# Half-head scores between projections, a later fill, routing copies on VectorE, and index digits in PSUM

## The chip, the core and the metric

The program runs on one core of a Trainium2 chip. TensorE (PE in the profile) multiplies matrices, its weight loads have a row of their own (PEld); VectorE (DVE) and ScalarE (ACT) work element by element and can read and write PSUM, where TensorE leaves its sums; GpSimd (POOL) works on SBUF, and it also issues the gathers by index; SyncE (SP) issues most of the plain loads. Each engine takes its instructions in the order of its own queue and waits on semaphores for the others. The metric is the time of one execution on the device, in microseconds (us).

## The reference

One layer of an encoder block over 512 tokens of width 1024, in float32. A mixing part (a spatial gating group beside a banded attention group) is added to the input. Then comes PEER, a product-key mixture of 16384 one-row experts. It is the second part that the change touches:

```python
q = (xb @ w_query).reshape(PEER_TOKEN_BLOCK, PEER_HEADS, 2, PEER_HALF)
sc = jnp.einsum('thpd,hpkd->thpk', q, sub_keys).astype(jnp.float32)
s_top, i_top = lax.top_k(sc, PEER_TOPK)
cand = s_top[:, :, 0, :, None] + s_top[:, :, 1, None, :]
cand_idx = i_top[:, :, 0, :, None] * PEER_NKEYS + i_top[:, :, 1, None, :]
best, pos = lax.top_k(cand.reshape(...), PEER_TOPK)
eidx = jnp.take_along_axis(cand_idx.reshape(...), pos, axis=-1)
g = jax.nn.softmax(best, axis=-1)
h = jax.nn.gelu(jnp.einsum('thkd,td->thk', expert_u[eidx], xb))
return jnp.einsum('thk,thkd->td', g * h, expert_v[eidx])
```

For each token and each of 8 heads a query of two halves is scored against two sets of 128 keys. The 16 best keys of each half give candidate pairs, and the 16 best pairs name 16 experts of that head, with a softmax gate for each.

## The kernel before

The tokens are four tiles of 128. One tile is handled by gathering the rows of its experts. The other three are handled densely: every expert's product with every token is made on TensorE in 128 blocks of 128 experts, and multiplied by a gate matrix that is zero where an expert was not chosen. Float32 operands are split into a high part `hi` (a rounded copy, by ScalarE) and a rest `lo` (a subtraction, by VectorE or GpSimd), and a product is three matmuls (`mm3`). For 64 of the dense tokens the first products are not made densely either; their expert rows are gathered early (`gather_early`, tile `rowe`) and reduced by VectorE (`dots_early`, called dots below).

The program has four stages after one another: the mixing part, the routing, the gate steps, and the second products with the gathered tile beside them. The change touches the routing and the gate steps.

**Routing** (the loop over `h` after `candidates`). For head `h` the weights of the query are loaded and split (two `lo` on GpSimd), and TensorE makes the projection of both halves (48 matmuls of 512 columns). Then come `FILL[h]` blocks of first products (24 matmuls of 320 columns each, one `lo` on GpSimd each), the first of them ahead of the scores. Then come the scores of both halves in one go, and ScalarE copies them out (`scr`, `s0`). VectorE finds the 16 best of each half for three token tiles (`top16` in `best_keys`). One round later `pairs` forms the candidates, with three small copies on ScalarE for heads 0 to 5 and on VectorE for heads 6 and 7, and `choose` takes the 16 best pairs and looks their indices up through six bit masks in PSUM and a tree of predicated copies, which ends in `eidx`. Two rounds after a head's scores GpSimd casts its indices and issues six gathers. After head 7 come eight more blocks of first products (`BRIDGE`), the softmax of all gates, and `indices_of`, which takes the index digits of one tile apart in integer arithmetic in SBUF (`ii`) and writes them back as floats. A scheduler that works by priority and readiness sets the order on each engine here; `issue_after` only adds edges.

**Gate steps** (the loop `for n in range(steps + LEAD)`, an order written out by hand). Each of 48 steps handles 8 tokens: `second_one_hot` on GpSimd makes `bm`, `first_one_hot` on VectorE makes `am`, and two steps later TensorE multiplies them (`products`). ScalarE copies the product to `gst`, and every second step a 1 MB store to DRAM follows. Between them stand a quarter of a block of first products per step, dots, gathers, splits (`split_next`, two of three on VectorE and the third on GpSimd), and twice `indices_of` for the next token tile. `gates_of` transposes the digits and gates on TensorE into a PSUM bank that VectorE reads for 16 steps.

PSUM tiles `pa` share four banks in both stages, and `pu`, for the first products, has two.

Of the kernel before, what the change touches and what calls it, by code (L numbers as in the profile page):

```python
# [8 lines left out]
F32 = mybir.dt.float32  # L9
# [62 lines left out]
FILL = (2, 2, 2, 2, 3, 3, 3, 3)  # L72
# [20 lines left out]
def hybrid_block(tc, x, ln1, w_in, gng, wsT, bsb, qkg, bias, w_out, ln2, wq, skT, uT, ud, vd, out):  # L93
    nc = tc.nc
    ctx = ExitStack()
    with ctx:
# [18 lines left out]
        iota_k = const.tile([P, P], F32, name="iota_k")  # L115
        nc.gpsimd.iota(iota_k, pattern=[[1, P]], base=0, channel_multiplier=0,
# [610 lines left out]
        def top16(val, pos, src, scratch):  # L727

            nc.vector.max(val[:, 0:8], src)
            nc.vector.max_index(pos[:, 0:8], val[:, 0:8], src)  # L730
            nc.vector.match_replace(scratch, val[:, 0:8], src, LOW)
            nc.vector.max(val[:, 8:16], scratch)
            nc.vector.max_index(pos[:, 8:16], val[:, 8:16], scratch)
# [6 lines left out]
        def best_keys(pool, top, pos, u, p2, src):  # L740
            rep = pool.tile([P, NK], F32, name="rep", tag="rep", bufs=2)
            top16(top[:, 0, u, p2, :], pos[:, u, p2, :], src, rep)
# [26 lines left out]
        def choose(pool, cand, n, best, to, mask, tree, spread=nc.gpsimd.tensor_copy):  # L769
# [7 lines left out]
            for i in range(6):  # L777
                nc.vector.tensor_scalar(mask[:, i * n * TOPK:(i + 1) * n * TOPK], bpos.rearrange("p t k -> p (t k)"),
                                        1 << i, None, op0=ALU.bitwise_and)
            mask = mask.rearrange("p (l t k) -> p l t k", t=n, k=TOPK)  # L780
            for i in reversed(range(6)):
# [20 lines left out]

        def candidates(h):

            if h:
                w = chunk_of(wq, h, eng=nc.gpsimd)
            else:
                with queued_behind(behind_norm):
                    w = chunk_of(wq, h)
            skt = rq.tile([P, 2, NK], F32, name="skt", tag="skt", bufs=2)  # L810
            nc.sync.dma_start(skt, skT[:, 2 * h:2 * h + 2, :])
            top, pos = keys(rq, ND)
            qts = []
            for p2 in range(2):
                ps = pa()
                for k in range(KT):
                    mm3(ps, w(k, slice(p2 * P, (p2 + 1) * P)), (xbh[:, k, :], xbl[:, k, :]),
                        k == 0, k == KT - 1)
                qt = rq.tile([P, S], F32, name="qt", tag="qt", bufs=2)
                nc.scalar.copy(qt, ps)  # L820
                qts.append(qt)
            fill = first_products(sum(FILL[:h]) + BC, FILL[h], nc.gpsimd, True)
            next(fill, None)
            s0 = rq.tile([P, 2, NK], F32, name="s0", tag="s0", bufs=2)
            for p2 in range(2):
                sp = pa()
                for t in range(TT):
                    nc.tensor.matmul(sp[:, t * P:(t + 1) * P], qts[p2][:, t * P:(t + 1) * P],
                                     skt[:, p2, :], start=True, stop=True)
                sc = rq.tile([P, ND, NK], F32, name="scr", tag="scr", bufs=2)  # L830
                nc.scalar.copy(sc, sp.rearrange("p (t n) -> p t n", n=NK)[:, GT:, :])
                nc.scalar.copy(s0[:, p2, :], sp[:, 0:NK])
                for t in range(ND):
                    best_keys(rq, top, pos, t, p2, sc[:, t, :])
            nc.scalar.dma_start(s0d[h], s0.rearrange("p a n -> p (a n)"))
            for _ in fill:
                pass
            return top, pos


        def indices_of(t):

            ii = gat.tile([P, 3, NH * TOPK], I32, name="ii", tag="ii", bufs=1)
            ff = ii.bitcast(F32)
# [4 lines left out]
            nc.vector.tensor_scalar(ei, ei, BL - 1, None, op0=ALU.bitwise_and)  # L849
            nc.vector.tensor_copy(ff, ii)  # L850
# [10 lines left out]
        cands = []  # L861
        for h in range(NH + 1):
            dots_early(0)
            if h < NH:
                cands.append(candidates(h))
            else:
# [358 lines left out]
```

## Time and profile before

| | |
|---|---|
| median of 3 runs | 1438.37 us (1434.36 to 1438.52) |
| profiled execution, own time | 1439.93 us |
| its span, first to last instruction | 1438.1 us |
| granted TensorE clock, mean | 0.990 |
| PE, DVE, POOL, ACT busy in the span | 1395.6, 1160.8, 703.3, 612.3 us |
| routing, 224 to 454 us: PE, DVE, POOL busy | 217.17, 185.59, 167.89 of 230 us |
| gate steps, 454 to 610 us: PE, DVE, POOL busy | 135.20, 131.93, 122.07 of 156 us |
| second products, from 610 us: PE busy | 822.84 of 828.1 us |

Rows of a timeline read: start, duration, engine, line, operation, output and inputs, shapes, count, and in brackets the idle time of the engine just before with what ended it. Rows of a table of groups give the count after an x, then the busy time and the mean of one in ns, then the idle time before. Rows of a table of waits give the time in total, how often, and the longest. Records of neighbouring instructions overlap a little, since an engine starts one while the last drains; so what an instruction costs in a row of its kind is the distance from start to start.

### The profile page before, as it was taken

How to read it: one execution, taken by the hardware profiler on the slowest of the kernel's cores; microseconds unless marked ns; L12 is line 12 of the kernel's file. 1: busy time of each engine (PE TensorE's matmuls, PEld its weight loads, DVE VectorE, ACT ScalarE, POOL GpSimd, SP SyncE). 2: the span in 40 equal slices, each digit the busy share in tenths (PEclk: the TensorE clock that was granted, in tenths of full speed). 3: DMA queues.
4: the chain of work that ended last, by engine and by line, in shares of the span. 5: the costliest groups of instructions: out<-in, count | busy, mean ns of one | idle time of the engine just before them, and what ended most of it. 6: DMA issues, size and time to landing. Idle time of an engine off the chain costs nothing.

```text
span 1438.1 us, 21787 instructions
## 1 busy us (share of the span) xinstructions
PE 1395.6 (97%) x7838; PEld 1233.5 (86%) x7838; DVE 1160.8 (81%) x2558; ACT 612.3 (43%) x975; POOL 703.3 (49%) x479
## 2 busy tenths in 40 slices
PE   9999999999988897899999999999999999999998
PEld 7887788998988887899898899898998998888887
DVE  5537753688999989689999999899879888688883
ACT  5447635443433444554434444343433333333331
POOL 0002104588778897514454556556545455254520
PEclk9999999999999999999999999999999999999999
DMA  4452226478667997879799999999989989789981
GB/s 164 129 191 74 89 103 206 137 263 280 230 212 233 300 326 231 272 264 351 285 354 360 335 351 367 346 399 363 388 328 360 358 328 366 260 328 352 350 325 62
DMA packets 164331, 396.25 MB, mean 276 GB/s; under 512 B 12880, under 2 KB 75232, under 8 KB 162176
## 3 DMA queue, kind: packets, MB, share of 16 engines
q1 hardware_dynamic: 64640, 194.14, 37.6%
q0 software_dynamic: 48176, 173.46, 32.9%
q10 hardware_dynamic: 51408, 27.27, 6.5%
q8 instruction: 61, 1.00, 0.3%
q14 instruction: 46, 0.38, 0.1%
HBM read 363.34 MB, written 31.46 MB: 275 GB/s over the span
## 4 chain that ended last, share of the span: by engine, by line
PE 74%; DVE 13%; DMA 6%; ACT 3%; POOL 2%; issue 2%; POOLq 0%; ACTq 0%; DVEq 0%; SPq 0%
PE pa L1145 21%; PE px L1145 11%; PE pu L189 9%; PE pu L190 9%; PE pu L191 9%; PE pa L189 4%; PE pa L190 3%; PE pa L191 3%; DMA gd<-gst 3%; DVE lo L152 2%; PE pa L956 2%; DVE row L1086 1%; DVE am L948 1%; DMA gc<-gd 1%; DVE acc L1097 1%
## 5 line engine op out<-in xcount | busy, mean ns | idle before, releaser
L151 ACT ACTIVATE hi<-raw 128x1024 fp32r<-128x1024 f32 x296 | 312.5, 1058 | 443.7 <-DMA raw<-in_vd 116.0
L152 DVE TENSOR_TENSOR lo<-raw,hi 128x1024 fp32r<-128x1024 f32 x243 | 302.7, 1247 | 79.8 <-ACT hi L151 79.2
L1084 POOL DMA_INDIRECT row<-in_ud,eint x128 | 199.5, 1559 | 172.7 <-DVE acc L1097 107.4
L1095 POOL DMA_INDIRECT row<-in_vd,eint x128 | 185.6, 1450 | 172.3 <-DVE row L1086 120.7
L189 PE MATMUL pu<-xch,hi 128*128 128x320 f32 x784 | 247.5, 316 | 1.2 <-ACT act L713 1.2
L190 PE MATMUL pu<-xcl,hi 128*128 128x320 f32 x784 | 242.5, 309 | 0.0
L191 PE MATMUL pu<-xch,lo 128*128 128x320 f32 x784 | 242.1, 309 | 0.0
L1145 PE MATMUL pa<-hi,wh 128*128 128x512 f32 x512 | 199.8, 390 | 0.0
L1145 PE MATMUL pa<-lo,wh 128*128 128x512 f32 x512 | 199.3, 389 | 0.0
L152 POOL TENSOR_TENSOR lo<-raw,hi 128x1024 fp32r<-128x1024 f32 x53 | 126.5, 2405 | 92.9 <-ACT hi L151 92.1
L1097 DVE SCALAR_TENSOR_TENSOR acc<-row,hw,acc 128x1024 f32<-128x1024 f32 x128 | 164.9, 1288 | 1.4 <-DMA row<-in_vd,eint 1.2
L1086 DVE SCALAR_TENSOR_TENSOR row<-row,xb 128x1024 f32<-128x1024 f32 x128 | 157.5, 1233 | 2.3 <-DMA row<-in_ud,eint 2.3
L1145 PE MATMUL pa<-hi,wl 128*128 128x512 f32 x512 | 158.2, 389 | 0.0
L189 PEld LDWEIGHTS pu<-xch,hi 128*128 128x128 f32 x784 | 148.3, 189 | 4.3 <-ACT act L713 2.9
L190 PEld LDWEIGHTS pu<-xcl,hi 128*128 128x128 f32 x784 | 148.3, 189 | 1.5
L191 PEld LDWEIGHTS pu<-xch,lo 128*128 128x128 f32 x784 | 148.1, 189 | 0.0
L956 PE MATMUL pa<-bm,am 128*128 128x128 f32 x768 | 99.0, 282 | 16.4 <-DVE am L948 8.7
L1145 PEld LDWEIGHTS pa<-hi,wl 128*128 128x128 f32 x512 | 96.1, 188 | 20.4
L1145 PEld LDWEIGHTS pa<-hi,wh 128*128 128x128 f32 x512 | 96.1, 188 | 20.3
L1145 PEld LDWEIGHTS pa<-lo,wh 128*128 128x128 f32 x512 | 96.1, 188 | 20.1
L956 PEld LDWEIGHTS pa<-bm,am 128*128 128x128 f32 x768 | 94.1, 197 | 20.6 <-issue 9.1
L1145 PE MATMUL px<-hi,wh 128*128 128x512 f32 x256 | 100.7, 393 | 4.2 <-ACT hi L151 4.2
(236 smaller groups left out, 2661.1 us busy)
## 6 DMA issues: line engine op xcount, KB each, us to landing
raw<-in_uT SPq DMA_DIRECT2D x128, 512.0 KB, 5.6
raw<-in_vd SPq DMA_DIRECT2D x128, 512.0 KB, 6.1
gd<-gst ACTq DMA_DIRECT2D x24, 1024.0 KB, 7.5
gc<-gd SPq DMA_DIRECT2D x15, 1280.0 KB, 8.5
raw<-in_w_in SPq DMA_DIRECT2D x19, 512.0 KB, 4.4
raw<-in_wq SPq DMA_DIRECT2D x16, 512.0 KB, 3.6
raw<-in_w_out SPq DMA_DIRECT2D x8, 512.0 KB, 3.6
gc<-gd SPq DMA_DIRECT2D x15, 256.0 KB, 10.3
```

The source lines that it names most:

```text
L151: nc.scalar.activation(hi, raw, AF.Copy)
L152: ins = eng.tensor_tensor(lo, raw, hi.bitcast(F32), op=ALU.subtract)
L189: nc.tensor.matmul(ps, lh[0], rh[0], start=first, stop=False)
L190: nc.tensor.matmul(ps, lh[0], rh[1], start=False, stop=False)
L191: nc.tensor.matmul(ps, lh[1], rh[0], start=False, stop=last)
L948: nc.vector.tensor_tensor(am, iota_k[:, None, :].to_broadcast(full), g[:, 0, c * TC:(c + 1) * TC, None].to_broadcast(full), op=ALU.is_equal)
L956: nc.tensor.matmul(ps[:, i * P:(i + 1) * P], am[:, 4 * q + i, :], bm[:, 4 * q + i, :], start=True, stop=True)
L1084: nc.gpsimd.indirect_dma_start(out=row, out_offset=None, in_=ud, in_offset=bass.IndirectOffsetOnAxis(ap=eint[:, j:j + 1], axis=0))
L1086: nc.vector.scalar_tensor_tensor(row, row, 1.0, xb0, op0=ALU.mult, op1=ALU.mult, accum_out=hw[:, j:j + 1])
L1095: nc.gpsimd.indirect_dma_start(out=row, out_offset=None, in_=vd, in_offset=bass.IndirectOffsetOnAxis(ap=eint[:, j:j + 1], axis=0))
L1097: nc.vector.scalar_tensor_tensor(acc0, row, hw[:, j:j + 1], acc0, op0=ALU.mult, op1=ALU.add)
L1145: nc.tensor.matmul(accs[t][half], (wh, wh, wl)[k][:, b, tok], w[b][k % 2][:, ds_], start=first and k == 0, stop=last and k == 2)
```

## The change

The code of routing is cut into two generators: `projected_keys(h, p2)` makes the projection of half a head and pauses in its middle, and `best_of(h, p2)` makes that half's scores and its 16 best keys. `candidates(h)` puts the scores of the half before into that pause: those of head `h-1`, half 1, amid the projection of head `h`, half 0, and those of half 0 amid the projection of half 1. Only the last head's second half has a block of first products in between. `scr` gets four buffers instead of two. The fill goes from two blocks per head, then three, to 0, 1, 2, 3, 4, 4, 3, 3, the sum being 20 as before. The dots of a round are queued behind that round's last `top16`. The copies of `pairs` are on VectorE for all heads. The six bit masks, one `tensor_scalar` each, become one `tensor_tensor` of `bpos` with a constant tile `bits`; this holds for the gathered tile too, where `choose` runs once per head. `indices_of` works in a PSUM bank and writes floats to a tile of its own. In the gate steps nothing is split in steps 0 and 1, and in steps 2 to 5 GpSimd makes all splits.

```diff
-FILL = (2, 2, 2, 2, 3, 3, 3, 3)
+FILL = (0, 1, 2, 3, 4, 4, 3, 3)
...
-            for i in range(6):
-                nc.vector.tensor_scalar(mask[:, i * n * TOPK:(i + 1) * n * TOPK], bpos.rearrange("p t k -> p (t k)"),
-                                        1 << i, None, op0=ALU.bitwise_and)
             mask = mask.rearrange("p (l t k) -> p l t k", t=n, k=TOPK)
+            nc.vector.tensor_tensor(mask, bpos[:, None, :, :].to_broadcast([P, 6, n, TOPK]),
+                                    bits[:, :, None, None].to_broadcast([P, 6, n, TOPK]), op=ALU.bitwise_and)
...
+            ps = pa()
+            for k in range(KT):
+                if k == KT // 2:
+                    yield
+                mm3(ps, weights_q[h](k, slice(p2 * P, (p2 + 1) * P)), (xbh[:, k, :], xbl[:, k, :]),
+                    k == 0, k == KT - 1)
...
+            sc = rq.tile([P, ND, NK], F32, name="scr", tag="scr", bufs=4)
+            nc.scalar.copy(sc, sp.rearrange("p (t n) -> p t n", n=NK)[:, GT:, :])
...
             for p2 in range(2):
+                for _ in projected_keys(h, p2):
+                    if p2:
+                        best_of(h, 0)
+                    elif h:
+                        best_of(h - 1, 1)
             fill = first_products(sum(FILL[:h]) + BC, FILL[h], nc.gpsimd, True)
+            if h == NH - 1:
+                next(fill, None)
+                best_of(h, 1)
...
-            ii = gat.tile([P, 3, NH * TOPK], I32, name="ii", tag="ii", bufs=1)
-            ff = ii.bitcast(F32)
+            ii = pa()[:, 0:3 * NH * TOPK].bitcast(I32).rearrange("p (i k) -> p i k", i=3)
...
+            ff = gat.tile([P, 3, NH * TOPK], F32, name="ff", tag="ff", bufs=1)
...
-            dots_early(0)
             if h < NH:
-                cands.append(candidates(h))
+                candidates(h)
+            with queued_behind(found):
+                dots_early(0)
...
-                    cand = pairs(rq, *cands.pop(0), ND, ps[:, 6 * ND * TOPK:8 * ND * TOPK], h >= NH - 1)
+                    cand = pairs(rq, *top_pos.pop(h - 1)[:2], ND, ps[:, 6 * ND * TOPK:8 * ND * TOPK], True)
...
-                while split < (AHEAD - LAST) * BC + HELD and len(ready) < HELD:
-                    split_next(nc.vector if split % 3 else nc.gpsimd)
+                if n > 1 and split < (AHEAD - LAST) * BC + HELD and len(ready) < HELD:
+                    split_next(nc.vector if split % 3 and n > 5 else nc.gpsimd)
```

Three places show how the order moves. The first is VectorE at the end of the choice of a middle head, where the masks are made (`bpos` holds the positions of the best pairs, `tree` the indices being looked up, the rows at L659 are dots). Before:

```order
L778 TENSOR_SCALAR pa<-bpos 128x48 x5
L659 SCALAR_TENSOR_TENSOR rowe,du<-rowe,px 128x1024
L778 TENSOR_SCALAR pa<-bpos 128x48
L788 COPY_PREDICATED tree<-pa,cand 128x48x18
L659 SCALAR_TENSOR_TENSOR rowe,du<-rowe,px 128x1024
L788 COPY_PREDICATED tree<-pa,tree 128x48x16
L659 SCALAR_TENSOR_TENSOR rowe,du<-rowe,px 128x1024
L788 COPY_PREDICATED tree<-pa,tree 128x48x8
```

And now, lines being three further down:

```order
L736 MAX_INDEX bpos<-gate,rep_2421 128x8
L781 TENSOR_TENSOR pa<-bpos,bits 128x288
L790 COPY_PREDICATED tree<-pa,cand 128x48x18
L790 COPY_PREDICATED tree<-pa,tree 128x48x16
L790 COPY_PREDICATED tree<-pa,tree 128x48x8
L790 COPY_PREDICATED tree<-pa,tree 128x48x4
L790 COPY_PREDICATED tree<-pa,tree 128x48x2
L790 COPY_PREDICATED tree<-pa,tree 128x48
L792 COPY eidx<-tree 128x3x16
```

Six masks became one instruction, and for heads 0 to 5 the predicated copies, each of which needs the one before, stand alone, with nothing between them.

The second place is VectorE at the start of the gate steps (`hb` and `lb` are digits as one-hot rows, `lo` is the split). Before:

```order
L929 TENSOR_TENSOR hb<-iota_k,pa 128x128
L932 TENSOR_TENSOR hb<-hb,pa 128x128
L929 TENSOR_TENSOR lb<-iota_k,pa 128x256
L152 TENSOR_TENSOR lo<-raw,hi 128x1024
L948 TENSOR_TENSOR am<-iota_k,pa 128x1024 x2
```

And now:

```order
L950 TENSOR_TENSOR hb<-iota_k,pa 128x128
L953 TENSOR_TENSOR hb<-hb,pa 128x128
L950 TENSOR_TENSOR lb<-iota_k,pa 128x256
L969 TENSOR_TENSOR am<-iota_k,pa 128x1024 x2
```

The split ahead of the second and third `am` is gone.

The third place is GpSimd from the last head's indices (`eui`) into the first gate steps. Before:

```order
L666 CAST eui<-eidx 64x8
L650 DMA rowe<-in_ud,eui 128x1024
L152 TENSOR_TENSOR lo<-raw,hi 128x1024
L940 TENSOR_TENSOR bm<-hb,lb 128x1024
L650 DMA rowe<-in_ud,eui 128x1024
L152 TENSOR_TENSOR lo<-raw,hi 128x1024
L940 TENSOR_TENSOR bm<-hb,lb 128x1024
L650 DMA rowe<-in_ud,eui 128x1024
L940 TENSOR_TENSOR bm<-hb,lb 128x1024 x2
```

And now:

```order
L669 CAST eui<-eidx 64x8
L961 TENSOR_TENSOR bm<-hb,lb 128x1024
L653 DMA rowe<-in_ud,eui 128x1024
L961 TENSOR_TENSOR bm<-hb,lb 128x1024
L653 DMA rowe<-in_ud,eui 128x1024
L961 TENSOR_TENSOR bm<-hb,lb 128x1024
L155 TENSOR_TENSOR lo<-raw,hi 128x1024
L961 TENSOR_TENSOR bm<-hb,lb 128x1024
L653 DMA rowe<-in_ud,eui 128x1024
L155 TENSOR_TENSOR lo<-raw,hi 128x1024
L961 TENSOR_TENSOR bm<-hb,lb 128x1024
L653 DMA rowe<-in_ud,eui 128x1024
```

The first three `bm` come sooner, and three splits follow one another between the third and the sixth `bm`, where one stood between the first and the second.

More of the change, by code (lines that the diff above doesn't have):

```diff
@@ L115, in hybrid_block @@
         iota_k = const.tile([P, P], F32, name="iota_k")
+        bits = const.tile([P, 6], U32, name="bits")
+        for i in range(6):
+            nc.gpsimd.memset(bits[:, i:i + 1], 1 << i)
         nc.gpsimd.iota(iota_k, pattern=[[1, P]], base=0, channel_multiplier=0,
@@ L732, in top16 @@
             nc.vector.max(val[:, 8:16], scratch)
-            nc.vector.max_index(pos[:, 8:16], val[:, 8:16], scratch)
+            return nc.vector.max_index(pos[:, 8:16], val[:, 8:16], scratch)
         def keys(pool, n):
@@ L741, in best_keys @@
             rep = pool.tile([P, NK], F32, name="rep", tag="rep", bufs=2)
-            top16(top[:, 0, u, p2, :], pos[:, u, p2, :], src, rep)
+            return top16(top[:, 0, u, p2, :], pos[:, u, p2, :], src, rep)
         def pairs(pool, top, pos, n, ps=None, own=False):
@@ L801, in softmax @@
             nc.vector.tensor_tensor(best, ex, zs[:, :, None].to_broadcast(full), op=ALU.mult)
-        def candidates(h):
[L805 to L813, printed above, removed]
-            for p2 in range(2):
[L815 to L821, printed above, removed]
-            fill = first_products(sum(FILL[:h]) + BC, FILL[h], nc.gpsimd, True)
[L823 to L835, printed above, removed]
@@ new lines, in hybrid_block, with projected_keys @@
+        weights_q, top_pos, qts, found = {}, {}, {}, []
+        def projected_keys(h, p2):
+            if p2 == 0:
+                if h:
+                    weights_q[h] = chunk_of(wq, h, eng=nc.gpsimd)
+                else:
+                    with queued_behind(behind_norm):
+                        weights_q[h] = chunk_of(wq, h)
+            ps = pa()
[4 more added lines that the diff above has]
+                    k == 0, k == KT - 1)
+            qts[h, p2] = rq.tile([P, S], F32, name="qt", tag="qt", bufs=2)
+            nc.scalar.copy(qts[h, p2], ps)
@@ new lines, in best_of @@
+        def best_of(h, p2):
+            if p2 == 0:
+                skt = rq.tile([P, 2, NK], F32, name="skt", tag="skt", bufs=2)
+                nc.sync.dma_start(skt, skT[:, 2 * h:2 * h + 2, :])
+                s0 = rq.tile([P, 2, NK], F32, name="s0", tag="s0", bufs=2)
+                top_pos[h] = (*keys(rq, ND), skt, s0)
+            top, pos, skt, s0 = top_pos[h]
+            qt = qts.pop((h, p2))
+            sp = pa()
+            for t in range(TT):
+                nc.tensor.matmul(sp[:, t * P:(t + 1) * P], qt[:, t * P:(t + 1) * P],
+                                 skt[:, p2, :], start=True, stop=True)
+            sc = rq.tile([P, ND, NK], F32, name="scr", tag="scr", bufs=4)
+            nc.scalar.copy(sc, sp.rearrange("p (t n) -> p t n", n=NK)[:, GT:, :])
+            nc.scalar.copy(s0[:, p2, :], sp[:, 0:NK])
+            for t in range(ND):
+                ins = best_keys(rq, top, pos, t, p2, sc[:, t, :])
+            found[:] = [getattr(ins, "ins", ins)]
+            if p2:
+                nc.scalar.dma_start(s0d[h], s0.rearrange("p a n -> p (a n)"))
```

5 lines of the change are left out of this document (2 added, 3 removed).

## The prediction, made before the changed kernel ran

> **What bounds the kernel now.** I read the windows of the three stages first (duration, then PE, PEld, DVE, ACT and POOL busy, granted clock, DMA share, GB/s).
>
> ```profile
> 224.00:454.00 230.00, 217.17 (x1272) 201.00 (x1270) 185.59 (x847) 93.90 (x159) 167.89 (x111) 0.98 0.65 221
> 454.00:610.00 156.00, 135.20 (x1034) 130.50 (x1034) 131.93 (x187) 69.08 (x120) 122.07 (x75) 0.96 0.91 280
> 610.00:1438.10 828.10, 822.84 (x4320) 729.06 (x4320) 713.36 (x1246) 326.99 (x469) 395.51 (x265) 1.00 0.88 330
> ```
>
> From 610 us PE is busy 822.84 of 828.10 us, and the change takes no product away there. So it can only shift the moment at which that stage begins. Before it PE is idle 12.8 us of routing and 20.8 us of the gate steps: about 34 us are the most to be had, and a little more where the clock dips. The table of waits of the gate steps says what ends them (total, times, longest).
>
> ```profile
> ACT gst L959 <- DMA gd<-gst: 31.9, 12, 4.8
> ...
> PE pa L956 <- DVE am L948: 8.7, 7, 4.6
> ...
> PE pa L918 <- DVE ii L850: 2.6, 2, 2.1
> ```
>
> The longest of PE's, 4.6 us for `am`, lies at the border of routing and gate steps and ends a chain. DVE's timeline shows that chain from its first key (L729) to the last one-hots.
>
> ```profile
> 241.30 0.49 DVE L729 MAX8 top<-scr 128x8 f32<-128x128 f32 x2 [16.49 <-ACT scr L831]
> ...
> 279.85 0.49 DVE L729 MAX8 top<-scr 128x8 f32<-128x128 f32 x2 [3.02 <-ACT scr L831]
> ...
> 428.96 1.21 DVE L788 COPY_PREDICATED tree<-pa,cand 128x864 f32<-128x864 uint32 x1
> 430.20 2.89 DVE L788 COPY_PREDICATED tree<-pa,tree 128x768 f32<-128x768 uint32 x5
> ...
> 434.67 0.23 DVE L846 CAST ii<-eidx 128x128 int32<-128x128 f32 x1
> ...
> 435.02 2.23 DVE L847 TENSOR_SCALAR ii<-ii 128x128 int32<-128x128 int32 x1
> ...
> 440.20 0.35 DVE L850 CAST ii<-ii 128x384 f32<-128x384 int32 x1
> ...
> 446.39 0.41 DVE L929 TENSOR_TENSOR lb<-iota_k,pa 128x256 f32<-128x256 f32 x1
> 448.08 5.30 DVE L152 TENSOR_TENSOR lo<-raw,hi 128x1024 fp32r<-128x1024 f32 x1 [1.27 <-ACT hi L151]
> ```
>
> After head 2's scores (279.85) DVE is never again late for want of scores: it works through its list until the digits are ready (L850 ends at 440.55), idle only where gathered rows are late for the dots:
>
> ```profile
> L659 DVE SCALAR_TENSOR_TENSOR rowe<-rowe,px 128x1024 f32<-128x1024 f32 x42 | 50.9, 1216 | 9.9 <-DMA rowe<-in_ud,eui 9.9
> ```
>
> So the gate steps' begin is set by DVE's late start, its list, and one `lo` of 5.30 us, where 1.2 us is what an instruction on 1024 elements takes (a dot's 1216 ns). PE and POOL at that place:
>
> ```profile
> 454.66 1.62 PE L956 MATMUL pa<-bm,am 128*128 128x128 f32 x6 [4.55 <-DVE am L948]
> ```
>
> ```profile
> 448.03 2.38 POOL L152 TENSOR_TENSOR lo<-raw,hi 128x1024 fp32r<-128x1024 f32 x1
> 450.37 1.92 POOL L940 TENSOR_TENSOR bm<-hb,lb 128x1024 f32<-128x1024 f32 x1
> ```
>
> DVE's `lo` starts 0.05 us after POOL's and ends at 453.38, 1.1 us after POOL's two instructions (452.29), its own length: it stands through both. L847, SBUF on both sides, takes 2.23 us, L846 of the same size 0.23. I call this standing.
>
> **The change part by part.**
>
> *Half scores and the later fill.* PE's rows give its pace.
>
> ```profile
> 224.78 0.40 PE L189 MATMUL pa<-xbh,hi 128*128 128x512 f32 x1
> ...
> 234.99 0.30 PE L189 MATMUL pu<-xbh,hi 128*128 128x320 f32 x1
> ...
> 238.51 1.95 PE L828 MATMUL pa<-skt,qt 128*128 128x128 f32 x16
> 240.21 0.39 PE L189 MATMUL pu<-xbh,hi 128*128 128x320 f32 x1
> ```
>
> 224.78 to 234.99 holds 45 of the 48 matmuls of head 0's projection, 0.227 us each, so it began at 224.1. The 24 of a block take 3.52 us, the scores of a head 1.70, of a half 0.85. Head 0's first half scores now come after 36 matmuls, at 224.1 + 8.2 = 232.3 instead of 238.51; with the 2.8 us from there to the first key (238.51 to 241.30) DVE starts at 235, 6 us earlier. More counts at head 2, from which on scores were not waited for: its first half comes after 132 matmuls, one block and four half scores, 224.1 + 30.0 + 3.5 + 3.4 = 261.0. DVE takes it at about 265 (2.8 for the copy, a little for its own backlog) instead of 279.85: 15 us earlier.
>
> *DVE's list from there.* From 279.85 to 440.55 are 160.7 us, 9.9 of it waiting for gathered rows, 150.8 of work. What changes in it:
>
> ```profile
> L778 DVE TENSOR_SCALAR pa<-bpos 128x48 uint32<-128x48 uint32 x48 | 10.0, 209 | 0.9
> ```
>
> ```profile
> L750 DVE COPY pa<-top x2: 203/282/361, 404.8 to 416.9; 128x48 f32<-128x48 f32 x2
> L752 DVE TENSOR_SCALAR pa<-pos x2: 199/199/199, 411.9 to 417.2; 128x48 f32<-128x48 uint32 x2
> L753 DVE CAST top<-pos x2: 172/178/184, 388.8 to 417.5; 128x48 f32<-128x48 uint32 x2
> ```
>
> - The copies of `pairs` (shortest, median and longest in ns above, now of heads 6 and 7) for the five further heads that fall in this time: 0.28 + 0.20 + 0.18 = 0.66 each, +3.3.
> - Six masks of 0.21 (1.25 a head) become one instruction on 288 elements; L929 on 256 takes 0.41, so 0.45. It saves 0.8 for each of seven heads, −5.6.
> - The predicated copies need one another's results, and dots no longer lie between them. Alone they take 4.1 us (428.96 to 433.09); between dots a part of that was filled. Bounds 0 and 1.5 a head; I take 0.85, the middle: +6.0.
> - `indices_of` works in PSUM: L847 without its standing, −2.0. Its bank is shared with the products' and costs nothing here, where those have not begun.
> - The new mask has both inputs in SBUF, and one copy of `pairs` (L753) goes from SBUF to SBUF. The trace has no instruction with the mask's operands. From below the price is 0: L778, also from `bpos` into PSUM, never stood (mean 209). From above stands an instruction with two SBUF inputs in the gate steps:
>
> ```profile
> 561.98 7.63 DVE L680 TENSOR_TENSOR gate<-gate,dots 64x128 f32<-64x128 f32 x1
> ```
>
> With L152's 5.30 that is 5 to 7 us a head at worst. POOL splits in this stage (its window above: busy 167.89 of 230 us, gathers included), mostly single splits of 2.4 us with a wait between them, and an instruction that meets one loses half of it on average. I take 1.0 a head, +7.0.
> - The 9.9 us of late rows stay: dots come later, but so do the gathers' indices.
>
> Sum: 150.8 + 9.9 + 3.3 − 5.6 + 6.0 − 2.0 + 7.0 = 169.4. The digits are ready at 265 + 169.4 = 434.4 instead of 440.55: only 6 of the 15 us are left.
>
> *From the digits to the first product.* It took 454.66 − 440.55 = 14.1 us, with three dots, the one-hots and the `lo` that stands. The dots are now behind, the `lo` gone. One-hots and `bm` need 1.1 (three small ones up to L929's) + 1.92. PE has 0.45 of `gates_of` and then some 36 matmuls of 0.147 (3.52/24) before the product, 5.3, the longer of the two. With up to a microsecond for a low clock: 6.6. The first product starts at 441, a gain of 13.5.
>
> Could PE be there sooner? Up to 454.66 it idled 13.5 us (12.8 in the window, 0.66 behind it), and the clock of 0.98 cost 2% of 230, 4.6: without either it would be there at 436.6. So the stalls of routing go into a new one of 4 to 5 us, PE's `gates_of` (L939 now) on the digits; all products stand behind it in PE's queue, so it is real.
>
> *The gate steps.* Two of the three splits that DVE made in steps 2 to 4 are now POOL's, 2.4 each (the `lo` above): +4.8 on an engine that is busy 122.07 of 156 us and whose `bm` every product needs. From below 0, since POOL has 34 us of idle time. From above the whole 13.5: the earlier products meet a DMA share of 0.91, and ACT's `gst` waits 31.9 us on stores. Since three splits in a row stand between `bm` of steps 2 and 5, I take them in full: +5. The later two index blocks escape their standing, and with it goes PE's wait for them (L918), −2.6 at most.
>
> ```profile
> 485.05 4.48 DVE L849 TENSOR_SCALAR ii<-ii 128x128 int32<-128x128 int32 x1
> ```
>
> The six memsets of `bits` lie at the program's start, long ahead of any routing on POOL, and the gathered tile's masks in the last stage, where PE is busy 99% of the time: nothing for both; without that cover the masks would save 0.8 for each of eight heads.
>
> Net: −13.5 + 5 − 2.6 = −11. The profiled execution took 1439.93, so 1429; the median of the runs lies 1.6 lower, so 1428.
>
> The Trainium skill ("SBUF — State Buffer", section "Who interferes with whom") has a rule for standing: VectorE's instructions with two SBUF inputs, and its copies, casts and tensor_scalars in a two-port mode, share a port pair with GpSimd under an exclusive lock, and operands in PSUM do not. L152, L680 and L847 agree with their 5.30, 7.63 and 2.23 us. By the rule the digits in PSUM are safe, and the new mask, with two SBUF inputs, is not, which is rival A.
>
> **The rivals.**
>
> *A, slower: the masks stand through POOL's work.* If every mask waits as L152 and L680 did, a head costs several us more, and the predicated copies, `eidx`, the gathers and dots of that head are queued behind it on DVE, so nothing fills the hole. At 4 us a head instead of 1 the digits come 21 us later, at 455, the first product at 462, 7.3 later than before; with 2.4 from the gate steps that is 1438.4 + 9.7 = 1448. The gain is gone once the digits come after 454.66 − 6.6 − 2.4 = 445.7 (2.6 a head). For it: the rows of 5.30 and 7.63. Against: both were met where POOL ran two instructions or more back to back; in routing it mostly has gaps.
>
> *B, the gate steps take it back.* If stores and POOL set the pace from 454 on, an earlier entry only waits longer. For it: 31.9 us and the share of 0.91. Against: PE's own waits there name `am` first and not `gst`. Then the index blocks' 2.6 are left: 1438.4 − 2.6 = 1436.
>
> *C, better: PE becomes the bound of routing.* Without standing (−7.0) the digits are ready at 427.4 and PE's 436.6 decides: a gain of 18, less 2.4, 1438.4 − 15.6 = 1423. Against: it needs the predicated copies at no more than counted, and rows no later than now.
>
> **How the numbers follow.** Chances: forecast 0.50, A 0.15, B 0.20, C 0.15. A difference of 0.3%, 4.3 us, is about what a measurement of this kernel can tell from none. Faster by that (under 1434.1): the forecast but for its slowest tenth, 0.45, C with 0.15, a quarter of B, 0.05: 0.65. Slower (over 1442.7): A, and a little of B, 0.17. Between them 0.18. The forecast's own range is 1421 to 1435 (standing between 0 and 2 a head, the gate steps between 0 and 9). The range for 8 in 10 goes from 1417 (C with gate steps that cost nothing) to 1440 (B with splits that cost more); it leaves out A.
>
> **What would show it.** Right, if the first `top<-scr` starts near 235 and DVE's long idle time at the start is gone; if PE's idle time in routing falls to about 5 us, most of it one wait for the digits; if the one mask (L781) takes about 0.45 us, now and then a few; if the digit instructions (L866 to L871) take 0.2 to 0.5 each at all three places; if the first product starts near 441, and the last stage 11 us earlier. Wrong, if the digits come after 445 (A), if the first product is early and the last stage is not (B), or if PE never waits for the digits (C).

## The result: slower by 1.1%

The changed kernel takes 1457.24 us (median of 4 runs, 1450.76 to 1462.42) against 1437.92 for the one before; the ratio is 1.0111, with a 95% interval of 1.0080 to 1.0141. The forecast was 1428 in a range of 1417 to 1440. The profiled execution took 1450.76 us, 10.8 more than the profiled one of before. It is the fastest of the four, so the traces show 10.8 us of a difference that is about 16 by the ratio.

The windows of the three stages, in the same cuts as before (duration, then PE, PEld, DVE, ACT, POOL busy, granted clock, DMA share, GB/s):

```profile
224.00:454.00 230.00, 212.50 (x1203) 193.82 (x1202) 207.12 (x806) 89.08 (x135) 157.02 (x104) 0.96 0.64 211
454.00:610.00 156.00, 138.80 (x1072) 134.21 (x1072) 118.76 (x194) 69.09 (x120) 133.67 (x80) 0.97 0.90 277
610.00:1449.00 839.00, 829.45 (x4353) 735.67 (x4351) 719.72 (x1218) 331.12 (x475) 395.10 (x268) 1.00 0.89 329
```

In routing PE does less than before (212.50 of 230 us busy, 217.17 before), and DVE is busy 21.5 us longer. The group of DVE that grew is the new mask:

```profile
L781 DVE TENSOR_TENSOR pa<-bpos,bits 128x288 uint32<-128x288 uint32 x8 | 31.8, 3971 | 1.4 <-DVE bpos L736 1.3
```

Its durations, shortest, median and longest in ns, are 459, 5192 and 6095:

```profile
L781 DVE TENSOR_TENSOR pa<-bpos,bits x8: 459/5192/6095, 252.7 to 445.6; 128x288 uint32<-128x288 uint32 x8
```

So 0.46 us is its own length, as estimated, and 31.8 − 8 × 0.46 = 28.1 us were spent standing. Two of the places, on POOL and on DVE:

```profile
296.01 7.08 POOL L155 TENSOR_TENSOR lo<-raw,hi 128x1024 fp32r<-128x1024 f32 x3
...
327.47 7.03 POOL L155 TENSOR_TENSOR lo<-raw,hi 128x1024 fp32r<-128x1024 f32 x3
```

```profile
297.35 6.08 DVE L781 TENSOR_TENSOR pa<-bpos,bits 128x288 uint32<-128x288 uint32 x1 [0.87 <-DVE bpos L736]
303.54 1.24 DVE L790 COPY_PREDICATED tree<-pa,cand 128x864 f32<-128x864 uint32 x1
...
328.74 6.09 DVE L781 TENSOR_TENSOR pa<-bpos,bits 128x288 uint32<-128x288 uint32 x1 [0.43 <-DVE bpos L736]
```

POOL's three splits end at 303.09 and 334.50, the masks at 303.43 and 334.83: both times 0.33 us after the third split. In these two places the mask does not slip in between two splits. It met splits in six of the eight heads and left a run of them before its end only once:

```profile
268.39 7.36 POOL L155 TENSOR_TENSOR lo<-raw,hi 128x1024 fp32r<-128x1024 f32 x3
```

```profile
271.02 2.48 DVE L781 TENSOR_TENSOR pa<-bpos,bits 128x288 uint32<-128x288 uint32 x1
```

Here it ended 0.33 us after the second split (273.18), and the third took 2.61 us instead of 2.4. The `hi` that this third split needs was ready only 0.06 us before the mask began; what decides whether the mask gets in was not tested. And PE waits for the end of the choice behind the mask:

```profile
307.73 0.52 PE L835 MATMUL pa<-skt,qt 128*128 128x128 f32 x1 [3.46 <-issue]
```

Its scores need a `pa` bank; the predicated copies, which read the mask from such a bank, begin at 303.54 and are through at 307.63. There are four such waits, 11.1 us in all; each ends 0.10 us after the last predicated copy, and in the runs below whose masks do not stand (`e1`, `e2`) there is none. This wait stands nowhere in the prediction:

```profile
PE pa L835 <- issue: 11.1, 4, 4.5
```

The first keys, the end of the digits, PE's transposes of them, the first product, the beginning of the last stage and one stall within it:

```profile
234.38 0.49 DVE L732 MAX8 top<-scr 128x8 f32<-128x128 f32 x2 [9.77 <-ACT scr L838]
...
457.88 0.56 DVE L871 CAST ff<-pa 128x384 f32<-128x384 int32 x1
```

```profile
458.54 0.87 PE L939 MATMUL pa<-ident,ff 128*128 128x128 f32 x3 [3.24 <-issue]
...
465.58 0.38 PE L977 MATMUL pa<-bm,am 128*128 128x128 f32 x2
...
618.33 0.77 PE L1166 MATMUL px<-hi,wh 128*128 128x512 f32 x1 [3.52 <-DMA raw<-in_vd]
...
775.40 0.63 PE L194 MATMUL pu<-xch,lo 128*128 128x320 f32 x1 [2.13 <-DVE lo L155]
```

The keys start where they were forecast, the digits are ready at 458.4 where 434.4 was forecast and 440.55 stood before. The last stage begins at 618.33 instead of 610.08, 8.25 us later, and is itself 2.6 us longer, with a stall at 775 that the kernel before did not have.

### The profile page after: what moved, and what is told of

It reads as the page before. It is cut to its first block, busy times and chain, and to the rows that moved or that the text cites. A ratio compares the mean times of both kernels' runs of the same rounds, so it can differ in the third digit from the quotient of the medians.

```text
span 1449.0 us, 21703 instructions
## 1 busy us (share of the span) xinstructions
PE 1400.5 (97%) x7838; PEld 1235.8 (85%) x7838; DVE 1175.7 (81%) x2494; ACT 612.0 (42%) x957; POOL 703.8 (49%) x487
## 4 chain that ended last, share of the span: by engine, by line
PE 68%; DVE 17%; DMA 6%; POOL 4%; issue 4%; ACT 2%; another core or an unknown queue 0%; POOLq 0%; ACTq 0%; SPq 0%; DVEq 0%
PE pa L1166 21%; PE px L1166 11%; PE pu L194 8%; PE pu L192 8%; PE pu L193 8%; PE pa L977 3%; PE pa L192 3%; DVE rowe L662 2%; PE pa L193 2%; POOL bm L961 2%; PE pa L194 2%; DVE pa L781 2%; DVE tree L790 2%; DVE lo L155 2%; DVE row L1107 2%
## 5 line engine op out<-in xcount | busy, mean ns | idle before, releaser
L155 DVE TENSOR_TENSOR lo<-raw,hi 128x1024 fp32r<-128x1024 f32 x241 | 296.1, 1231 | 74.8 <-ACT hi L154 74.0
L1105 POOL DMA_INDIRECT row<-in_ud,eint x128 | 205.5, 1606 | 191.7 <-DVE acc L1118 128.6
L1116 POOL DMA_INDIRECT row<-in_vd,eint x128 | 176.3, 1378 | 160.7 <-DVE row L1107 103.6
L155 POOL TENSOR_TENSOR lo<-raw,hi 128x1024 fp32r<-128x1024 f32 x55 | 131.2, 2398 | 100.3 <-ACT hi L154 99.7
```

The lines of the kernel that those rows point to most:

```text
L155: ins = eng.tensor_tensor(lo, raw, hi.bitcast(F32), op=ALU.subtract)
L1105: nc.gpsimd.indirect_dma_start(out=row, out_offset=None, in_=ud, in_offset=bass.IndirectOffsetOnAxis(ap=eint[:, j:j + 1], axis=0))
L1116: nc.gpsimd.indirect_dma_start(out=row, out_offset=None, in_=vd, in_offset=bass.IndirectOffsetOnAxis(ap=eint[:, j:j + 1], axis=0))
```

## The experiments

The runs were made in four groups, each on one chip beside the kernel before, and a run's ratio to it is what counts; the kernel before had medians of 1440.57 to 1441.94 in them. Moments are read from one profiled run of each kernel. `e2`, `e11`, `e13` and `e15` have the same routing on every engine, and their digits are ready at 443.3, 440.9, 444.4 and 443.9 us; so a difference of up to 3.5 us between two traces says nothing by itself.

### The mask's operands: six masks, bits in PSUM, and the mask alone

`e1` undoes the mask:

```diff
-            nc.vector.tensor_tensor(mask, bpos[...], bits[...], op=ALU.bitwise_and)
+            for i in range(6):
+                nc.vector.tensor_scalar(mask[:, ...], bpos.rearrange("p t k -> p (t k)"), 1 << i, None, op0=ALU.bitwise_and)
```

> The changed kernel with one part undone: the mask is again six tensor_scalar instructions, everywhere. Theory standing (rival A): in the changed kernel the one mask took 31.8 us for eight heads where 0.46 is its own length, 28 us too much, and the scores' wait for its bank is a result of it. Then six masks of 0.21 take 10 us without any standing, the digits are ready 20 to 24 us earlier (434 to 438 instead of 458), the first product at 441 to 444 instead of 465.6, and the time falls by about 22 us from the changed kernel's 1457, to 1430 to 1437. Theory list: the later dots and the copies on VectorE make the list longer, and the masks only fill holes; then 1445 to 1455 remains, and DVE shows new idle time where the masks stood.

Ratio 1.0025 (1.0003 to 1.0047), 1444.87 us.

`e2` keeps the one instruction and moves its constant for the dense tiles; the gathered tile's stays in SBUF (lines are cut at `...`):

```diff
+                mbits = ps[:, 8 * ND * TOPK:8 * ND * TOPK + 6].bitcast(U32)
+                nc.scalar.copy(mbits, bits)
...
-                                    bits[:, :, None, None].to_broadcast([P, 6, n, TOPK]), op=ALU.bitwise_and)
+                                    (bits if mbits is None else mbits)[:, :, None, None].to_broadcast([P, 6, n, TOPK]), op=ALU.bitwise_and)
```

> The changed kernel with the same one mask instruction, but its constant operand in PSUM: ScalarE copies the six bits beside the mask in its bank, once per head. So only one of the two inputs is in SBUF. Theory standing by two SBUF inputs: all eight masks take 0.4 to 0.6 us, the digits are ready at about 430, the first product at 437 to 440, 1422 to 1432. If it is the instruction itself that stands beside POOL (its shape, or its output in PSUM), masks still take up to 6 us and the time stays at 1450 to 1460. Theory list: masks short, and yet 1445 to 1455.

Ratio 1.0037 (1.0014 to 1.0060), 1446.18 us. Its masks (shortest, median, longest in ns):

```profile
L781 DVE TENSOR_TENSOR pa<-bpos,pa x8: 448/461/464, 253.7 to 431.8; 128x288 uint32<-128x288 uint32 x8
```

Same operation, same shape, a split of POOL running beside each of the eight and in the four middle heads another right behind it, and not one stands. So it was the second input in SBUF, and not the instruction, its output or its place. PE's queue holds the same work in the same order as in the changed kernel, and POOL's too, save two gathers that moved ahead of the last indices but one. Of the 1.1% the mask of the dense tiles was 0.7. The first theory's times were missed by both: 1430 to 1437 and 1422 to 1432 were given, 1445 and 1446 measured, about what the theory of a longer list gave. The digits came at 444.2 and 443.3, so VectorE's list was longer than I thought even without standing, and the digits no earlier than before (440.55).

`e3` puts the one mask, bits in SBUF, into the kernel before:

> The kernel before with one part of the change alone: one mask instruction with bits in SBUF in place of six. Theory standing: in this order too POOL splits for more than half of routing, several masks take 2 to 6 us, 12 to 25 us in all, and since VectorE sets the end of routing there, the time rises by 5 to 20 us, to 1443 to 1458. If the standing needs the change's own order (gathers that hold POOL until three splits run in a row), masks take under 1.5 us on average and the time is 1432 to 1440.

Ratio 1.0078 (1.0056 to 1.0101), 1452.26 us, in the range of the first theory, but not for its reason alone. Its masks took 18.5 us, 14.8 too many, in a few long ones. The order that the planner (the scheduler of routing) makes changed too: it put three of a head's gathers and the next head's indices on POOL ahead of splits. The edit also holds for the gathered tile, which gets one mask as well (`e14` below has that alone, 0.17%). The next run takes the standing away and leaves the other two.

### The kernel before with a shorter list

`e8` takes `e3`, moves the bits into PSUM as in `e2`, and the digits too. POOL's queue holds the same order as in `e3`.

> The kernel before with the one mask instruction, its bits in PSUM, and the digits in PSUM; routing's order, the fill, the copies and the splits of the gate steps as before. VectorE's list is shorter by 4.8 (8.3 to 3.5 for masks) and 2 (L847): digits at 434 instead of 440.5, first product at 441 instead of 447.3. By the half that the gate steps take back the time is 1434 to 1437. If the begin of the gate steps does not matter at all (GpSimd sets their end): 1437 to 1441.

Ratio 1.0054 (1.0034 to 1.0073), 1448.82 us: still slower, by about 0.2% less than `e3` (the intervals overlap), though no mask stands and VectorE's own work from 224 us to the digits is 2.3 us less (distance from start to start, 170.4 against 172.7); its idle time is 6.2 us more (50.1 against 43.9), and the digits come at 444.5 instead of 440.55, hardly more than runs of one routing differ by. POOL, ACT and PE at the sixth and seventh head:

```profile
399.71 0.19 POOL L669 CAST eui<-eidx 64x8 int32<-64x8 f32 x1 [4.26 <-DMA rowe<-in_ud,eui]
...
403.96 6.97 POOL L155 TENSOR_TENSOR lo<-raw,hi 128x1024 fp32r<-128x1024 f32 x3
```

```profile
410.02 1.06 ACT L154 ACTIVATE hi<-raw 128x1024 fp32r<-128x1024 f32 x1 [12.49 <-DMA raw<-in_uT]
```

```profile
411.45 0.64 PE L192 MATMUL pu<-xbh,hi 128*128 128x320 f32 x1 [11.37 <-ACT act L716]
```

POOL waits for the next head's indices with three splits queued behind them. Those splits free the `raw` buffers, so the loads come late, ACT stands 12.49 us for one, its `act` copies behind that come late, and PE stands 11.37 us. That the buffers are the link is read from the order of events; no run isolated it. Of the 0.54% the gathered tile's one mask may be 0.17 (`e14`), which would leave about 0.4% for the order in routing.

`e10` asks the same with a larger dose, half of every dot left out:

```diff
-                nc.vector.scalar_tensor_tensor(row, row, 1.0, xbu, op0=ALU.mult, op1=ALU.mult,
+                nc.vector.scalar_tensor_tensor(row[:, :D // 2], row[:, :D // 2], 1.0, xbu[:, :D // 2], op0=ALU.mult, op1=ALU.mult,
```

> The kernel before with half of each dot left out (512 of 1024 columns, so the dots' values are not the right ones); the gathers stay whole. That takes about 0.55 us from each of the 39 dots ahead of the digits, 21 us of VectorE's list, and nothing else. If VectorE's list sets the begin of the gate steps, the digits come 5 to 15 us earlier than 440.5 (as far as late rows and PE let them), and if that begin matters fully, the last stage moves by as much, to 595 to 605. If the gate steps give half of it back, the last stage starts at 603 to 608 and the time is 1431 to 1436. If they give all back: 1437 to 1441 with the last stage near 610.

None of the three came. The ratio is 1.0130 (1.0089 to 1.0172), 1457.03 us: with 21 us less work VectorE is ready with the digits 18 us later, at 458.8. Waits in routing:

```profile
ACT hi L151 <- DMA raw<-in_uT: 68.7, 13, 12.5
DVE rowe L659 <- DMA rowe<-in_ud,eui: 41.1, 21, 6.7
```

Before, VectorE waited 9.9 us for gathered rows, and ACT 36.1 us for the loads. The planner again put gathers ahead of splits on POOL, five splits in a row behind them. So my premise, that VectorE's list sets the begin of the gate steps, does not hold by itself: VectorE, POOL's queue with gathers and splits, and the loads behind the splits form one loop, and shortening one of them gave nothing here; each time it also changed the order of the others.

### Parts of the changed routing

`e5` is `e2` with the copies of `pairs` of heads 0 to 5 given back to ScalarE, and `e6` is `e5` with the dots queued ahead of the projections again.

> The changed kernel with two parts undone or mended: the bits in PSUM as in the run before (masks no longer stand), and the three copies of pairs of heads 0 to 5 on ScalarE again. VectorE's time up to the digits, by the distance from start to start, held 8.2 us for the eight heads' copies in that run (5.2, 1.5 and 1.5), against 0.8 in the kernel before. Theory (VectorE's list sets the digits): they are ready 7 us earlier, at 436 instead of 443.3, the first product at 443 to 444; the gate steps take about half of such a gain back (first product 13 us later moved the last stage by 7 us between these runs), so 1440 to 1443. Rival: ScalarE is late with the copies (before, pairs waited for it) and VectorE stands idle instead: no change against 1446.

Ratio 1.0047 (1.0026 to 1.0067), 1449.2 us, against 1.0037 for `e2`. Not faster; what the rival named happened. VectorE's wait for scores, first in `e2`, then in `e5`:

```profile
DVE top L732 <- ACT scr L838: 16.6, 6, 9.5
```

```profile
DVE top L732 <- ACT scr L838: 30.7, 12, 9.9
```

The copies wait on ScalarE for VectorE's positions, and the scores of the next half stand behind them. So moving them back brings nothing, though they cost VectorE 8.2 us; the intervals of the two runs overlap, and which place is better is not shown.

> The run before (bits in PSUM, copies on ScalarE) and also the dots queued as in the kernel before, ahead of a round's projections and not behind its last top16. Theory: the late dots cost twice, 42 instead of 39 of them lie ahead of the digits (3.4 us), and GpSimd's gathers wait for their buffers with the splits queued behind them. Then the digits come at 431 to 434, PE's waits for a split (429.02, 4 us) go, and the time is 1434 to 1440. Rival: dots ahead of the top16 hold the keys up and VectorE loses at the start what it gains at the end; 1441 to 1446.

Ratio 1.0043 (1.0028 to 1.0059), 1447.08 us: no difference from `e2` or `e5` that these intervals separate, and not the gain I expected: the digits come at 441.3, where 431 to 434 was given. VectorE now waits for rows, 18.7 us in all, where `e2` waited 4.1:

```profile
DVE rowe L662 <- DMA rowe<-in_ud,eui: 18.7, 12, 5.7
```

`e12` is `e2` with only the fill set back, to two blocks a head and then three:

> The changed kernel with its bits in PSUM (1446 in an earlier call) and the fill of the kernel before, two blocks a head and then three. The third head's first scores then come three blocks, 10.6 us, later (273.6 instead of 263). If the earlier scores are of use, the digits come 5 to 10 us later than 443.3 and the time rises by 3 to 8, to 1449 to 1454. If they only move VectorE's idle time and its late dots around, it stays at 1444 to 1448, or falls, since GpSimd then has fewer splits in the later heads.

Ratio 1.0026 (1.0003 to 1.0049), 1445.77 us. The third head's keys start at 274.0 instead of 263.0, and the digits are ready at 444.1 instead of 443.3. Eleven microseconds at the start were worth 0.8 at the end, less than runs of the same routing differ by.

### The gate steps

`e4` puts the digits in PSUM and the new rule for the splits into the kernel before, and `e11` takes the rule out of `e2`:

```diff
-                if n > 1 and split < (AHEAD - LAST) * BC + HELD and len(ready) < HELD:
-                    split_next(nc.vector if split % 3 and n > 5 else nc.gpsimd)
+                while split < (AHEAD - LAST) * BC + HELD and len(ready) < HELD:
+                    split_next(nc.vector if split % 3 else nc.gpsimd)
```

> The kernel before with the other part alone: index digits in PSUM and no split in the first two gate steps, GpSimd's splits in steps 2 to 5. My own sum: the stall of 4.55 us before the first product and the 2.0 of L847 go, some 6 to 8 us at the entry; the index blocks 2.6; two splits more on POOL give 0 to 5 back: 1428 to 1436. Rival B (stores and POOL set the pace of the gate steps): 1436 to 1439.

> The changed kernel with its bits in PSUM (1446 in an earlier call) and the splits of the gate steps as in the kernel before: two of three on VectorE, from step 0 on. If the change's rule for the splits helps, the stall of 4.55 us in front of the second product comes back and the time is 1448 to 1452; if it costs (two more splits on GpSimd, three in a row), 1440 to 1444; if it is worth nothing, as in the kernel before, 1445 to 1448.

`e4`: 0.9997 (0.9976 to 1.0018), 1440.89 us. `e11`: 1.0048 (1.0026 to 1.0070), 1447.4 us. Alone and within the change this part is worth nothing that can be measured, and my own sum for `e4`, 1428 to 1436, was missed. The trace of `e4` says where the gain went. The stall of 4.55 us in front of the second step's product is gone, and so is the wait for the digits of later tiles (2.6 us before). But PE waits for `bm` instead, on GpSimd, which now makes the splits of steps 2 to 5. PE's waits from 446 to 600 us, before and in `e4`:

```profile
PE pa L956 <- DVE am L948: 8.7, 7, 4.6
PE pa L956 <- POOL bm L940: 5.4, 6, 2.4
```

```profile
PE pa L956 <- POOL bm L940: 12.8, 15, 2.5
...
PE pa L956 <- DVE am L948: 2.5, 3, 1.6
```

So 6.2 us of waits for VectorE became 7.4 us of waits for GpSimd, where the prediction had put 5.

`e9` leaves out half of POOL's one-hot work:

```diff
-            nc.gpsimd.tensor_tensor(bm.rearrange("p t (h l) -> p t h l", l=BL), ...
+            nc.gpsimd.tensor_tensor(bm[:, 0:TC // 2].rearrange("p t (h l) -> p t h l", l=BL), ...
```

> The kernel before with half of GpSimd's one-hot work left out: bm is made for four of a step's eight tokens and used for both halves, so each costs about 1 us instead of 2 and the gate matrix is not the right one; all else is as it was. If GpSimd sets the pace of the gate steps, the time from the first to the last product falls from 151 us to 130 to 140, and the last stage starts 10 to 20 us earlier. If the stores of gst or the DMA share of 0.91 set it, it stays within 5 us of 151 and ScalarE's wait for the stores grows.

One run: from the first to the last product 146.8 us (150.8 before; 141.4 to 151.1 in the other runs, all with the whole `bm`), the last stage at 609.8. POOL alone does not set the pace. Waits in the gate steps (446 to 600 us):

```profile
ACT gst L961 <- DMA gd<-gst: 46.0, 11, 10.3
...
PE pa L958 <- ACT gst L961: 15.8, 4, 7.1
```

ACT's wait for the stores grew from 31.9 to 46.0, and PE's wait for ACT's copies from 2.4 to 15.8. With half of POOL's one-hot work out of the way the waits on the stores grow. What a lighter store would do was not tried.

### The gathered tile's mask, and what is left

After `e2` 0.4% was left. Runs with one mask in the gathered tile had a stall of PE near 770 us, those with six had none. `e13` is `e2` with six masks there; `e14` is the kernel before with one there and nothing else:

```diff
+            if n < ND:
+                nc.vector.tensor_tensor(mask..., bpos[...], bits[...], op=ALU.bitwise_and)
-            for i in range(6):
+            for i in range(6 if n == ND else 0):
```

> The changed kernel with its bits in PSUM for the dense tiles (1446 in an earlier call), and for the gathered tile six masks again, as in the kernel before. In all runs with one mask there, TensorE stood 3.3 to 3.8 us near 770 us behind a split of VectorE, which stood behind a load of scores (sc), and ran at half clock after it; in the runs with six masks it did not. Theory (the shorter list of the gathered tile brings that load's reader to a worse place): the stall near 770 us goes and the time falls by 4 to 6, to 1440 to 1442. Rival (the stall follows from the late start of the last stage): it stays, 1445 to 1447.

> The kernel before with one mask instruction for the gathered tile alone; routing and gate steps untouched. Theory: the stall near 765 us appears here too, 1444 to 1447 against 1440.6. Rival: nothing changes, 1440 to 1441.

`e13`: 1.0013 (0.9990 to 1.0037), 1443.17 us. `e14`: 1.0017 (1.0001 to 1.0033), 1444.3 us. The times moved the expected way and by 2 to 3 us, a little less than I gave; the interval of `e14` only just leaves out 1, and that of `e13` overlaps with that of `e2`. In the trace the stall is gone in `e13`, and there in `e14`, on DVE and on PE:

```profile
763.75 0.49 DVE L732 MAX8 top<-sc 128x8 f32<-128x128 f32 x2 [3.64 <-DMA sc<-s0d]
```

```profile
768.32 0.63 PE L194 MATMUL pu<-xch,lo 128*128 128x320 f32 x1 [3.34 <-DVE lo L155]
```

VectorE comes to the next head's keys before their load is there, and the split that PE needs is queued behind them. The granted clock in `e14` is 1.00 from 755 to 765 us and 0.50 from 768 to 772, so the stall costs more than its 3.34 us. All nine kernels with one mask in the gathered tile have such a stall, of 2.1 to 3.6 us between 765 and 784 us, and none of the eight with six. But the profiled `e13` shows no shorter last stage (834.4 us, `e2` 834.0): PE stands 1.5, 1.4 and 2.0 us at other places there. Why five instructions fewer a head bring VectorE to this place was not followed further.

`e15` is `e13` with the old rule for the splits, and `e16` also has the old fill:

> The changed kernel with bits in PSUM, six masks in the gathered tile and the splits of the gate steps as before: what is left of the change is half scores, fill, copies, dots and digits. Its last stage began at 605 us in the run with old splits, against 610 before. If both parts add, 1437 to 1442; if this kernel is faster than the one before at all, by no more than 4.

> As the kernel with old splits and six gathered masks, and also the fill of the kernel before. The fill alone was worth nothing (digits at 444.1 against 443.3, 1445.8 against 1446.2), so within 3 of that kernel.

`e15`: 1.0012 (0.9990 to 1.0034), 1444.38 us, so the parts did not add to the 1437 to 1442 given; `e16`: 1.0038 (1.0016 to 1.0060), 1446.68 us, within 3 us of `e15`. No version beats the kernel before.

The decomposition, each from ratios to the kernel before:

| step | ratio after it |
|---|---|
| the change as it is | 1.0111 (1.0080 to 1.0141) |
| bits in PSUM for the dense tiles (`e2`) | 1.0037 (1.0014 to 1.0060) |
| and six masks for the gathered tile (`e13`) | 1.0013 (0.9990 to 1.0037) |
| and the old splits in the gate steps (`e15`) | 1.0012 (0.9990 to 1.0034) |

By the middle values about 10.7 us of the change's 16 are the mask of the dense tiles and about 3 that of the gathered tile (the intervals of these two rows overlap; `e14` says 0.17% for the same mask alone). The rest is not told apart from nothing.

## Why the prediction was wrong

**The bound of the last stage** held for its length as a whole (830.7 us after, 828.0 before, from its first product to the end), but "nothing" for the gathered tile's masks was most likely wrong. PE was busy 99% there, and yet one late split came with 0.17% (`e14`, 0.01 to 0.33). A busy engine did not mean that its inputs had time to spare.

**The earlier scores** came as worked out: first keys at 234.38 (235 forecast), third head's at 262.9 (265). What failed is "15 us earlier" as a gain at the end: `e12` takes 11 of them away, and the digits move by 0.8.

**The price of standing** is the step that failed by most. It was put at 1.0 us a head, because splits were "mostly single splits of 2.4 us with a wait between them, and an instruction that meets one loses half of it on average". It measured 28.1 us over eight heads, 3.5 each, 5.3 to 5.6 in the four middle heads that stood through three splits. Both halves of the reason were wrong. The trace of before shows runs of three splits in routing, five of them from 295 us on, most behind a head's gathers, a row that I did not read:

```profile
370.29 7.12 POOL L152 TENSOR_TENSOR lo<-raw,hi 128x1024 fp32r<-128x1024 f32 x3
```

And the meeting is no accident of phase: in the four middle heads the mask began 1.3 to 1.6 us after the first of the three splits. In the changed order a head's dots free the buffers for the gathers, the gathers stand ahead of the three splits on POOL, and the choice and its mask stand behind the dots on DVE. Both queues reach the place together, head after head. Rival A, at a chance of 0.15, was right in mechanism and place, and near in size: 4 us a head given, 3.5 measured. That its digits, 455, lie so near the 458.4 measured is partly luck. Without standing they came at 443.3 (`e2`), where its sum implies 427.4; and standing moved them by 15 us, not by the 28 that it adds up to, in part since VectorE's idle time on the way was 9.6 us with it and 18.2 without (`e13`). The term is most of the slowdown, but not all of the miss: without it the kernel is still no faster (`e2`, `e13`).

The Trainium skill's rule ("SBUF — State Buffer", section "Who interferes with whom"), quoted in the prediction, says which instruction stands, and the trace agrees: two inputs in SBUF stood up to 6.09 us (`after`), one in PSUM took 0.46 each time (`e2`). I named it and then gave the row of the older mask, which has a single input in SBUF, the greater weight. By the rule that row could not speak for the new mask.

**The rest of VectorE's list** was too short as well. From the third head's keys to the digits, in distances from start to start, the list without standing should have grown by 1.7 us; in `e13`, where no mask stands, it grew by 13.9 (149.1 to 163.0):

| VectorE, third head's keys to digits (us) | before | after | `e13` |
|---|---|---|---|
| masks | 7.1 | 31.1 | 3.0 |
| predicated copies | 22.3 | 26.0 | 25.5 |
| three copies of `pairs` | 0.8 | 4.6 | 7.2 |
| dots | 44.6 | 47.9 | 47.8 |
| all work | 149.1 | 185.9 | 163.0 |
| idle | 11.6 | 9.6 | 18.2 |

The masks' saving and the predicated copies' loss were the right sign and near enough (−4.1 against −5.6, +3.2 to +3.7 against +6.0). The copies cost up to twice what was given, since the cast among them (SBUF to SBUF) stood too, up to 1.99 us for 0.19 of its own. Two or three dots more lie ahead of the digits, which I had at nothing. Most of the rest are the keys and pairs (`top16`, 2.9 us more in `e13`) and two instructions of the softmax with both inputs in SBUF, which took 3.9 us instead of 1.1. And the idle time does not vanish with earlier scores; it comes back at other waits.

**From the digits to the first product** I read the wrong row. The product at 454.66 is not the first but that of the second step; the first one starts at 447.28:

```profile
447.28 0.38 PE L956 MATMUL pa<-bm,am 128*128 128x128 f32 x2
```

That is 6.7 us behind the digits, as the 6.6 that I gave to the new kernel (measured: 7.1). So this term could give no 7.5 us, only the stall of 4.55 us behind it, and what that gave was lost again at the next steps (`e4`).

**The gate steps** were to give 5 us back of 13.5. Moments of all profiled runs (us), in the order of their first product:

| run | first product | last stage |
|---|---|---|
| `e4` | 446.0 | 608.8 |
| before | 447.3 | 610.1 |
| `e11` | 448.3 | 605.0 |
| `e14` | 449.8 | 609.2 |
| `e9` | 450.6 | 609.8 |
| `e16` | 451.4 | 610.0 |
| `e15` | 451.5 | 608.6 |
| `e2` | 451.7 | 611.7 |
| `e13` | 451.9 | 610.2 |
| `e1` | 452.4 | 611.1 |
| `e12` | 452.7 | 608.5 |
| `e8` | 453.2 | 614.1 |
| `e6` | 454.3 | 613.6 |
| `e5` | 458.3 | 617.8 |
| after | 465.6 | 618.3 |
| `e10` | 467.1 | 623.4 |
| `e3` | 467.2 | 624.6 |

Up to an entry at 452.7 the last stage begins between 605.0 and 611.7, in no order with the first product. Beyond it moves, and in part. No run entered before 446.0, so what digits at 434.4 would have given is not shown; by this table the forecast of −11 would most likely not have come, and Rival B's mechanism would hold there. POOL is not what holds the stage alone (`e9`); that the stores hold it is what the waits suggest, not what a run isolated.

## What to carry to other kernels

When a change merges small instructions into one, look at where its operands lie and at what the neighbour engine has queued at that very moment: here two engines that the same event releases met in head after head, and an average over the stage said nothing of it. An engine with little idle time is not yet the bound; where it sits in a loop with queues and loads of others, less work for it can end later, as in `e8` and `e10`, where the planner's order on GpSimd changed with it. And before a sum is made, find the first instance of the thing that is timed: one row further down cost 7 us of forecast that were never there.

## What the runs showed of the hardware

- A VectorE instruction with two inputs in SBUF stood through three GpSimd instructions in a row, 6.08 and 6.09 us for an own length of 0.46, and ended 0.33 us after the third. Of its six meetings with splits in the changed kernel, it got in ahead of one that was still to come only once (2.48 us at 271.02).
- The same instruction with one of its inputs in PSUM took 448 to 464 ns in all eight cases, each with a split running beside it (`e2`). That its output lay in PSUM had not helped.
- Index arithmetic on 128 by 128 elements took 0.30 us in PSUM at all three places (after); in SBUF it had taken 0.21 to 4.48 (before).
- After a wait of TensorE of 3.34 us the granted clock was 0.50 from 768 to 772 us, where it was 1.00 in the kernel before (`e14`).
